# Attention on one core: Q and K of batches 1 to 7 transposed by the DMA crossbar instead of TensorE

## The chip, the core and the metric

The kernel runs on one core of a Trainium2 chip. Five engines of that core matter here: TensorE (PE, matmuls; its weight loads are listed as PEld), VectorE (DVE), ScalarE (ACT), GpSimd (POOL) and SyncE (SP). GpSimd and SyncE only issue DMAs in this kernel; 16 DMA engines move the data between HBM and SBUF, or inside SBUF. The metric is the device time of one execution in microseconds.

## The reference

The reference is plain attention without a mask, over 8 batches of 2048 rows with 512 columns, all float32.

```python
# q, k, v: (8, 2048, 512) float32
def reference(q, k, v):
    d_k = q.shape[-1]
    scores = np.matmul(q, k.transpose(0, 2, 1)) / np.sqrt(d_k)
    attn_weights = special.softmax(scores, axis=-1).astype(np.float32)
    return np.matmul(attn_weights, v)
```

## The kernel before

The batches are worked on one after another. A batch's 2048 rows are 16 blocks of 128 (NKB), its 512 columns four chunks of 128 (ND).

**Loads.** `prep_dma(b)` loads K, Q and V of a batch with GpSimd's DMAs (L62 to L64), which turn float32 into float16 on the way. K and Q come in two halves of eight blocks each, into the tiles `kh` and `qh`, of which there is one buffer each (`prep_pool`, bufs=1): the load of the next batch has to wait until the transposes of this one have read them. V comes into `vh`, with a column of ones behind it (L56), in two buffers.

**Transposes.** TensorE contracts over partitions, so the scores need Q and K with the columns (d) on the partitions. `prep_tr(b)` makes `qtT` and `ktT` from `qh` and `kh` (two buffers each). For each half, for K and then Q, and for each chunk of d, eight TensorE transposes against an identity matrix (L80) fill one PSUM tile `trp` (one buffer), and VectorE copies it to SBUF (L85). That is 16 groups of eight transposes for a batch.

**The main loop.** `main_batch(b)` goes over four query tiles (qt) of 512 rows. For each of them it does two stages:

- Scores: for each of the 16 key blocks four matmuls over the chunks of d (L98, 128 x 128 weights from `ktT`, 512 columns from `qtT`) give a tile `stp` in PSUM, and ScalarE writes exp of it, scaled, into `ptall` (L105). The softmax's maximum isn't subtracted.
- Output: for each of the four 128-row parts (qs) of the query tile, 16 pairs of matmuls (L117 with 257 columns, L121 with 256) sum exp times V, and through the column of ones the row sums, into a PSUM tile `op`, of which there are two buffers. VectorE takes the reciprocal of the sum (L126) and multiplies (L129) into `osb`, of which there are four buffers, and SyncE's queue stores it (L131).

`main_batch(b)` begins with `prep_dma(b + 1)`, and after query tile 1 it calls `prep_tr(b + 1)`. Batch 0 is loaded and transposed ahead of the loop.

**Order.** Each engine works its instructions in order, and so does each engine that issues DMAs: a DMA whose data isn't ready holds up the ones behind it in the same issuing engine's stream. The tile framework puts in the waits and may move instructions of one engine past each other by their readiness: in the trace the transposes of the next batch stand between the score matmuls of query tile 2, eight transposes to four score matmuls.

Of the kernel before, what the change touches and what calls it, by code (L numbers as in the profile page):

```python
# [1 line left out]

# [1 line left out]

# [5 lines left out]


@with_exitstack
def kernel(
    ctx: ExitStack,
    tc: tile.TileContext,
    q: bass.AP,
    k: bass.AP,
    v: bass.AP,
    out: bass.AP,  # L20
):
    nc = tc.nc
    P = 128
    B, T, D = q.shape
    F16 = mybir.dt.float16
    F32 = mybir.dt.float32

    NKB = T // P
    ND = D // P
    QTW = 512  # L30
    NQT = T // QTW
    NQS = QTW // P
    NB_ = 256
    NA_ = D + 1 - NB_
    inv_sqrt_d = float(1.0 / np.sqrt(D))
    GP = min(8, NKB)
    NG = NKB // GP

    const = ctx.enter_context(tc.tile_pool(name="const", bufs=1))
    prep_pool = ctx.enter_context(tc.tile_pool(name="prep", bufs=1))  # L40
    persist = ctx.enter_context(tc.tile_pool(name="persist", bufs=2))
    pt_pool = ctx.enter_context(tc.tile_pool(name="ptp", bufs=2))
    oout_pool = ctx.enter_context(tc.tile_pool(name="oout", bufs=4))
    st_psum = ctx.enter_context(tc.tile_pool(name="st_ps", bufs=3, space=bass.MemoryType.PSUM))
    o_psum = ctx.enter_context(tc.tile_pool(name="o_ps", bufs=2, space=bass.MemoryType.PSUM))
    tr_psum = ctx.enter_context(tc.tile_pool(name="tr_ps", bufs=1, space=bass.MemoryType.PSUM))

    ident = const.tile([P, P], F16)

    prepared = {}  # L50

    def prep_dma(b):
        qh = prep_pool.tile([P, NKB, D], F16, tag="qh")
        kh = prep_pool.tile([P, NKB, D], F16, tag="kh")
        vh = persist.tile([P, NKB, D + 1], F16, tag="vh")
        nc.vector.memset(vh[:, :, D:D + 1], 1.0)  # L56
        qsrc = q[b].rearrange("(n p) d -> p n d", p=P)
        ksrc = k[b].rearrange("(n p) d -> p n d", p=P)
        vsrc = v[b].rearrange("(n p) d -> p n d", p=P)
        for g in range(NG):  # L60
            ts = slice(g * GP, (g + 1) * GP)
            nc.gpsimd.dma_start(out=kh[:, ts, :], in_=ksrc[:, ts, :])  # L62
            nc.gpsimd.dma_start(out=qh[:, ts, :], in_=qsrc[:, ts, :])  # L63
        nc.gpsimd.dma_start(out=vh[:, :, 0:D], in_=vsrc)  # L64
        prepared[b] = [qh, kh, vh, None, None]

    def prep_tr(b):
        st = prepared[b]
        qh, kh = st[0], st[1]
        qtT = persist.tile([P, ND, T], F16, tag="qtT")  # L70
        ktT = persist.tile([P, ND, T], F16, tag="ktT")
        st[3] = qtT
        st[4] = ktT
        for g in range(NG):
            for src, dst in ((kh, ktT), (qh, qtT)):
                for dc in range(ND):
                    trp = tr_psum.tile([P, GP * P], F16, tag="trp")
                    for j in range(GP):
                        tb = g * GP + j
                        nc.tensor.transpose(  # L80
                            trp[:, j * P:(j + 1) * P],
                            src[:, tb, dc * P:(dc + 1) * P],
                            ident,
                        )
                    nc.vector.tensor_copy(  # L85
                        out=dst[:, dc, g * GP * P:(g + 1) * GP * P], in_=trp[:]
                    )

    def main_batch(b):
        if b + 1 < B:  # L90
            prep_dma(b + 1)
        _, _, vh, qtT, ktT = prepared[b]
        for qt in range(NQT):
            ptall = pt_pool.tile([P, NKB, QTW], F16, tag="ptall")
            for kb in range(NKB):
                stp = st_psum.tile([P, QTW], F32, tag="stp")
                for dc in range(ND):
                    nc.tensor.matmul(  # L98
                        stp[:],
                        ktT[:, dc, kb * P:(kb + 1) * P],  # L100
                        qtT[:, dc, qt * QTW:(qt + 1) * QTW],
                        start=(dc == 0),
                        stop=(dc == ND - 1),
                    )
                nc.scalar.activation(  # L105
                    out=ptall[:, kb, :],
                    in_=stp[:],
                    func=mybir.ActivationFunctionType.Exp,
                    scale=inv_sqrt_d,
                )  # L110
            for qs in range(NQS):
                op = o_psum.tile([P, 2 * 512], F32, tag="op")
                opA = op[:, 512:512 + NA_]
                opB = op[:, 0:NB_]
                for kb in range(NKB):
                    lhs = ptall[:, kb, qs * P:(qs + 1) * P]
                    nc.tensor.matmul(  # L117
                        opA, lhs, vh[:, kb, NB_:NB_ + NA_],
                        start=(kb == 0), stop=(kb == NKB - 1),
                    )  # L120
                    nc.tensor.matmul(  # L121
                        opB, lhs, vh[:, kb, 0:NB_],
                        start=(kb == 0), stop=(kb == NKB - 1),
                    )
                rinv = oout_pool.tile([P, 1], F32, tag="rinv")
                nc.vector.reciprocal(out=rinv[:], in_=op[:, 512 + NA_ - 1:512 + NA_])  # L126
                osb = oout_pool.tile([P, D], F32, tag="osb")
                src = op.rearrange("p (a c) -> p a c", c=512)[:, :, 0:NB_]
                nc.vector.tensor_scalar_mul(out=osb[:], in0=src, scalar1=rinv[:])  # L129
                gq = qt * NQS + qs  # L130
                nc.sync.dma_start(  # L131
                    out=out[b, gq * P:(gq + 1) * P, :], in_=osb[:]
                )
            if qt == min(1, NQT - 1) and b + 1 < B:
                prep_tr(b + 1)

    prep_dma(0)
    ident_dram = nc.inline_tensor(
        np.eye(P, dtype=np.float16), name="attn_identity"
    )  # L140
    nc.sync.dma_start(out=ident[:], in_=ident_dram.ap())
    prep_tr(0)
    for b in range(B):
        main_batch(b)


# [1 line left out]
_INS = ['q', 'k', 'v']  # L148
_OUTS = [((8, 2048, 512), 'float32')]


# [23 lines left out]
```

## Time and profile before

| what | value |
|---|---|
| median of the runs | 985.29 us |
| lowest of the runs | 985.02 us |
| span of the profiled execution | 983.6 us |
| granted TensorE clock, mean | 0.999 |
| TensorE busy | 963.9 us, 7168 matmuls and transposes |
| VectorE busy | 205.8 us |
| ScalarE busy | 306.7 us |
| HBM read, written | 100.70 MB, 33.55 MB |

The span runs from the first to the last instruction of one profiled execution, and its time on the device is slightly longer. In the groups of the page a row names the line, the engine and the operation, what is written and read with its shape, how often it ran, then its busy time in us, the mean of one in ns, and the idle time ahead of it with what ended it. In the rows of the timeline the first two numbers are the start and the length in us. In a row of DMA issues the last numbers are the size of one and the median time from issue to landing.

### The profile page before, as it was taken

How to read it: one execution, taken by the hardware profiler on the slowest of the kernel's cores; microseconds unless marked ns; L12 is line 12 of the kernel's file. 1: busy time of each engine (PE TensorE's matmuls, PEld its weight loads, DVE VectorE, ACT ScalarE, POOL GpSimd, SP SyncE). 2: the span in 40 equal slices, each digit the busy share in tenths (PEclk: the TensorE clock that was granted, in tenths of full speed). 3: DMA queues.
4: the chain of work that ended last, by engine and by line, in shares of the span. 5: the costliest groups of instructions: out<-in, count | busy, mean ns of one | idle time of the engine just before them, and what ended most of it. 6: DMA issues, size and time to landing. Idle time of an engine off the chain costs nothing.

```text
span 983.6 us, 15767 instructions
## 1 busy us (share of the span) xinstructions
PE 963.9 (98%) x7168; PEld 658.6 (67%) x7168; DVE 205.8 (21%) x392; ACT 306.7 (31%) x513; POOL 37.5 (4%) x44
## 2 busy tenths in 40 slices
PE   4999999999999999999999999999999999999998
PEld 3667766667666676666676766667666677666676
DVE  2214311142111421114111141112411123111111
ACT  0332233322233322233322233322333222333221
POOL 2100100001000000001000010000100000000000
PEclk9999999999999999999999999999999999999999
DMA  9991926009160192502934048521566110001111
GB/s 170 208 180 44 174 74 118 33 33 203 54 119 33 34 204 56 110 36 49 179 79 94 33 70 156 103 70 43 81 134 127 45 44 23 33 33 43 43 44 43
DMA packets 68435, 84.94 MB, mean 86 GB/s; under 512 B 2832, under 2 KB 51984, under 8 KB 68368
## 3 DMA queue, kind: packets, MB, share of 16 engines
q0 software_dynamic: 49792, 50.33, 32.2%
q1 hardware_dynamic: 18576, 33.60, 9.2%
q8 instruction: 56, 0.92, 0.4%
q14 instruction: 11, 0.09, 0.0%
HBM read 100.70 MB, written 33.55 MB: 136 GB/s over the span
## 4 chain that ended last, share of the span: by engine, by line
PE 98%; DMA 1%; DVE 1%; issue 0%; POOLq 0%
PE stp L98 45%; PE op L117 23%; PE op L121 23%; PE trp L80 7%; DMA kh<-in_k_dram 1%; DVE ktT L85 0%; DVE qtT L85 0%; DVE osb L129 0%; DVE rinv L126 0%; POOLq L159 0%
## 5 line engine op out<-in xcount | busy, mean ns | idle before, releaser
L105 ACT ACTIVATE ptall<-stp 128x512 f16<-128x512 f32 x512 | 305.5, 597 | 658.3 <-PE stp L98 658.3
L98 PE MATMUL stp<-qtT,ktT 128*128 128x512 f16 x2048 | 467.0, 380 | 0.0
L117 PE MATMUL op<-vh,ptall 128*128 128x257 f16 x2048 | 452.5, 273 | 0.0
L121 PE MATMUL op<-vh,ptall 128*128 128x256 f16 x2048 | 452.5, 272 | 0.0
L98 PEld LDWEIGHTS <-ktT 128*128 128x128 f16 x2048 | 195.6, 98 | 208.0 <-issue 0.6
L117 PEld LDWEIGHTS <-ptall 128*128 128x128 f16 x2048 | 198.8, 97 | 30.5
L121 PEld LDWEIGHTS <-ptall 128*128 128x128 f16 x2048 | 199.5, 97 | 28.8
L126 DVE RECIPROCAL rinv<-op 128x1 f32<-128x1 f32 x128 | 21.6, 168 | 672.0 <-PE op L121 672.0
L129 DVE TENSOR_SCALAR osb<-op,rinv 128x512 f32<-128x512 f32 x128 | 96.1, 751 | 4.5 <-DVE rinv L126 0.3
L80 PEld LDWEIGHTS <-kh 128*128 128x128 f16 x512 | 35.0, 100 | 31.1 <-issue 14.5
L85 DVE COPY ktT<-trp 128x1024 f16<-128x1024 f16 x64 | 44.2, 691 | 50.7 <-PE trp L80 50.7
L85 DVE COPY qtT<-trp 128x1024 f16<-128x1024 f16 x64 | 44.3, 692 | 46.3 <-PE trp L80 46.3
L80 PE MATMUL trp<-ident,kh 128*128 128x128 f16 x512 | 40.5, 224 | 13.7 <-DMA kh<-in_k_dram 10.3
L80 PEld LDWEIGHTS <-qh 128*128 128x128 f16 x512 | 34.9, 99 | 22.0 <-issue 14.8
L80 PE MATMUL trp<-ident,qh 128*128 128x128 f16 x512 | 40.1, 222 | 1.6 <-DVE ktT L85 0.8
L62 POOL DMA_DIRECT2D kh<-in_k_dram x16 | 14.2, 889 | 436.4 <-PE trp L80 435.6
L64 POOL DMA_DIRECT2D vh<-in_v_dram x8 | 9.2, 1153 | 248.3 <-DVE osb L129 207.1
L63 POOL DMA_DIRECT2D qh<-in_q_dram x16 | 14.0, 882 | 27.5 <-PE trp L80 27.5
L105 ACT ACT_TABLE_LOAD x1 | 1.3, 1283 | 0.7 <-PEq L159 0.7
L56 DVE MEMSET vh<- 128x16 f16 x8 | 0.6, 72 | 0.9 <-PEq L159 0.9
L159 POOL MEMSET const-float32-0.0<- 128x1 f32 x1 | 0.1, 98 | 0.2 <-issue 0.2
L159 POOL MEMSET const-bfloat16-1.0<- 128x1 bf16 x1 | 0.1, 101 | 0.0
(2 smaller groups left out, 0.2 us busy)
## 6 DMA issues: line engine op xcount, KB each, us to landing
out_dram<-osb SPq DMA_DIRECT2D x128, 256.0 KB, 2.0
kh<-in_k_dram POOLq DMA_DIRECT2D x16, 1024.0 KB, 14.2
qh<-in_q_dram POOLq DMA_DIRECT2D x16, 1024.0 KB, 21.5
vh<-in_v_dram POOLq DMA_DIRECT2D x8, 2048.0 KB, 14.8
ident<-attn_identity SPq DMA_DIRECT2D x1, 32.0 KB, 1.6
```

The source lines that it names most:

```text
L56: nc.vector.memset(vh[:, :, D:D + 1], 1.0)
L62: nc.gpsimd.dma_start(out=kh[:, ts, :], in_=ksrc[:, ts, :])
L63: nc.gpsimd.dma_start(out=qh[:, ts, :], in_=qsrc[:, ts, :])
L64: nc.gpsimd.dma_start(out=vh[:, :, 0:D], in_=vsrc)
L80: nc.tensor.transpose(trp[:, j * P:(j + 1) * P], src[:, tb, dc * P:(dc + 1) * P], ident,)
L85: nc.vector.tensor_copy(out=dst[:, dc, g * GP * P:(g + 1) * GP * P], in_=trp[:])
L98: nc.tensor.matmul(stp[:], ktT[:, dc, kb * P:(kb + 1) * P], qtT[:, dc, qt * QTW:(qt + 1) * QTW], start=(dc == 0), stop=(dc == ND - 1),)
L105: nc.scalar.activation(out=ptall[:, kb, :], in_=stp[:], func=mybir.ActivationFunctionType.Exp, scale=inv_sqrt_d,)
L117: nc.tensor.matmul(opA, lhs, vh[:, kb, NB_:NB_ + NA_], start=(kb == 0), stop=(kb == NKB - 1),)
L121: nc.tensor.matmul(opB, lhs, vh[:, kb, 0:NB_], start=(kb == 0), stop=(kb == NKB - 1),)
L126: nc.vector.reciprocal(out=rinv[:], in_=op[:, 512 + NA_ - 1:512 + NA_])
L129: nc.vector.tensor_scalar_mul(out=osb[:], in0=src, scalar1=rinv[:])
```

## The change

Q and K of batches 1 to 7 are no longer transposed by TensorE. `prep_tr(b)` for b > 0 issues eight transposing DMAs on SyncE's queue instead, SBUF to SBUF: four groups of four blocks (TG = 4), K and Q in turn, each with a source of 128 partitions x 2048 float16. Batch 0 is still transposed by TensorE, in groups of two blocks with all four chunks of d each.

`qtT` and `ktT` get another layout, [128, block, chunk, row in the block] instead of [128, chunk, row]; the score matmul's moving operand becomes four runs of 128 columns, 512 elements apart. The call of `prep_tr(b + 1)` moves from behind query tile 1 to behind query tile 0. Loads, output stage and stores stay as they are.

```diff
+    TG = 4
...
     def prep_tr(b):
         st = prepared[b]
         qh, kh = st[0], st[1]
-        qtT = persist.tile([P, ND, T], F16, tag="qtT")
-        ktT = persist.tile([P, ND, T], F16, tag="ktT")
+        qtT = persist.tile([P, NKB, ND, P], F16, tag="qtT")
+        ktT = persist.tile([P, NKB, ND, P], F16, tag="ktT")
         st[3] = qtT
         st[4] = ktT
-        for g in range(NG):
+        if b == 0:
+            for g in range(NG):
+                for src, dst in ((kh, ktT), (qh, qtT)):
+                    for j in range(0, GP, 2):
+                        tb = g * GP + j
+                        trp = tr_psum.tile([P, 2, ND, P], F16, tag="trp")
+                        for jj in range(2):
+                            for dc in range(ND):
+                                nc.tensor.transpose(
+                                    trp[:, jj, dc, :],
+                                    src[:, tb + jj, dc * P:(dc + 1) * P],
+                                    ident,
+                                )
+                        nc.vector.tensor_copy(out=dst[:, tb:tb + 2], in_=trp[:])
+            return
+        for g in range(NKB // TG):
+            ns = slice(g * TG, (g + 1) * TG)
             for src, dst in ((kh, ktT), (qh, qtT)):
-                for dc in range(ND):
-                    trp = tr_psum.tile([P, GP * P], F16, tag="trp")
-                    for j in range(GP):
-                        tb = g * GP + j
-                        nc.tensor.transpose(
-                            trp[:, j * P:(j + 1) * P],
-                            src[:, tb, dc * P:(dc + 1) * P],
-                            ident,
-                        )
-                    nc.vector.tensor_copy(
-                        out=dst[:, dc, g * GP * P:(g + 1) * GP * P], in_=trp[:]
-                    )
+                nc.sync.dma_start_transpose(
+                    out=dst[:, ns].rearrange("p n c r -> p (n c) r"),
+                    in_=src[:, ns, :].rearrange("p n d -> p (n d)"),
+                )
...
-                        ktT[:, dc, kb * P:(kb + 1) * P],
-                        qtT[:, dc, qt * QTW:(qt + 1) * QTW],
+                        ktT[:, kb, dc, :],
+                        qtT[:, qt * NQS:(qt + 1) * NQS, dc, :],
...
-            if qt == min(1, NQT - 1) and b + 1 < B:
+            if qt == 0 and b + 1 < B:
                 prep_tr(b + 1)
```

## The prediction

> **What bounds the kernel now.** I read the page's head and its chain of waits first, then the costliest groups.
>
> ```profile
> span 983.6 us, 15767 instructions
> PE 963.9 (98%) x7168; PEld 658.6 (67%) x7168; DVE 205.8 (21%) x392; ACT 306.7 (31%) x513; POOL 37.5 (4%) x44
> PE stp L98 45%; PE op L117 23%; PE op L121 23%; PE trp L80 7%; DMA kh<-in_k_dram 1%; DVE ktT L85 0%; DVE qtT L85 0%; DVE osb L129 0%; DVE rinv L126 0%; POOLq L159 0%
> ...
> L105 ACT ACTIVATE ptall<-stp 128x512 f16<-128x512 f32 x512 | 305.5, 597 | 658.3 <-PE stp L98 658.3
> ...
> L85 DVE COPY ktT<-trp 128x1024 f16<-128x1024 f16 x64 | 44.2, 691 | 50.7 <-PE trp L80 50.7
> ...
> L80 PE MATMUL trp<-ident,kh 128*128 128x128 f16 x512 | 40.5, 224 | 13.7 <-DMA kh<-in_k_dram 10.3
> ...
> L80 PE MATMUL trp<-ident,qh 128*128 128x128 f16 x512 | 40.1, 222 | 1.6 <-DVE ktT L85 0.8
> ```
>
> TensorE is the bound: 98% busy, and the chain of waits runs through it nearly end to end. Of that chain, 7% is L80, the 1024 transposes. The other engines are far away from it: ScalarE has 658.3 us of idle time, waiting for TensorE. So an instruction taken off TensorE in the steady part should come off the time whole. A busy sum is no price for it, since matmuls overlap; I take the price from stretches of batch 1, cut at the moments where VectorE begins the last reciprocal (L126) of a query tile (qt). The columns are the stretch, its length, then busy time and count of each engine, the granted clock, the DMA share and GB/s.
>
> ```profile
> 148.13:176.03 27.90, 27.90 (x193) 18.71 (x192) 3.71 (x10) 9.55 (x16) 1.15 (x1) 1.00 0.58 113
> 176.03:203.93 27.90, 27.90 (x196) 18.82 (x195) 3.68 (x9) 9.55 (x16) 0.00 (x0) 1.00 0.10 39
> 203.93:240.15 36.22, 36.22 (x321) 25.70 (x319) 14.65 (x25) 9.55 (x16) 3.49 (x4) 1.00 0.61 107
> ```
>
> A query tile without transposes takes 27.90 us, the one that holds the 128 transposes of the next batch 36.22 us; both at a granted clock of 1.00 and with TensorE never idle. One batch's transposes therefore cost 36.22 - 27.90 = 8.32 us, or 65 ns each.
>
> **The change part by part.** *Removed from TensorE:* the transposes of batches 1 to 7, 7 x 8.32 = 58.2 us, all of it on the path. The eviction copies of those batches go from VectorE too (112 x 0.69 us); VectorE is 21% busy, so that is worth nothing.
>
> *Batch 0* keeps 128 transposes and 16 evictions of the same size, in another order: two 128-row blocks with all four d chunks each, instead of one chunk of eight blocks.
>
> ```profile
> 12.13 1.01 PE L80 MATMUL trp<-ident,kh 128*128 128x128 f16 x8 [0.78 <-DVE ktT L85]
> ...
> 19.31 1.01 PE L80 MATMUL trp<-ident,qh 128*128 128x128 f16 x8 [0.78 <-DVE qtT L85]
> ...
> 20.12 1.48 PE L98 MATMUL stp<-qtT,ktT 128*128 128x512 f16 x3
> ```
>
> Before, the first score matmuls fill the gaps after six groups of eight. After, the first score tile needs the first K pair and two Q pairs, which is again the sixth group in order. I take 0; one or two groups earlier or later, at 1.79 us each (1.01 + 0.78), bound it at 3.6 us to either side.
>
> *The score matmul's moving operand* becomes four runs of 128 columns instead of one of 512. No row shows such an operand.
>
> ```profile
> 35.08 6.91 PE stp L98 x32
> ```
>
> This row of the chain gives 6.91 / 32 = 216 ns for the run of 512. Four separate 128-column matmuls at the 65 ns above would be 260 ns, so +44 ns x 2048 = 90 us is the upper end. The lower end is 0: TensorE issues these back to back and the columns stay as many. I take 0, as the same elements of the same partitions are streamed.
>
> *Added on SP's queue:* 8 transposing DMAs a batch, 56 in all, each 128 x 2048 f16 = 512 KB in and out of SBUF, placed behind the outputs of qt 0 and ahead of those of qt 1. Call the time of one T and of a batch X = 8T. No row shows a crossbar transfer; these are the nearest.
>
> ```profile
> DMA packets 68435, 84.94 MB, mean 86 GB/s; under 512 B 2832, under 2 KB 51984, under 8 KB 68368
> q0 software_dynamic: 49792, 50.33, 32.2%
> q1 hardware_dynamic: 18576, 33.60, 9.2%
> out_dram<-osb SPq DMA_DIRECT2D x128, 256.0 KB, 2.0
> kh<-in_k_dram POOLq DMA_DIRECT2D x16, 1024.0 KB, 14.2
> ident<-attn_identity SPq DMA_DIRECT2D x1, 32.0 KB, 1.6
> ```
>
> Lower end: the hardware queue's packets took 9.2% of 16 engines x 983.6 us = 1448 us for 33.60 MB, 371 GB/s when all 16 run; 512 KB at that rate is 1.4 us. Upper end: a 128x128 block of f16 is 32 KB in 128 rows of 256 bytes, just what the identity's load is, and that took 1.6 us; 16 such blocks, each waiting for the one before, are 25.6 us. Between them lies the store of 256 KB on the same queue: 2.0 us to landing, so 4.0 us for 512 KB as two of them. I take T = 4.0 us, X = 32 us, because that row is nearest in queue, engines and size, and both its latencies are already counted.
>
> Here two pages of the Trainium skill disagree. "DMA: Bandwidth & Descriptors" (section Latency and other measured facts) gives 261 GB/s for transposing DMAs whose middle dimension isn't contiguous; as an estimate that is T = 2.0 us, as hidden as mine. "VectorE: DVE Perf Modes" (section The three transpose paths) sets 1309 ns for a 128x128 block by the crossbar against 390 ns on TensorE, and would leave such a block to TensorE; 16 of those in a row are an estimate of 20.9 us. The identity's 1.6 us for one small DMA reads like such a figure: mostly latency, which 16 blocks in one DMA don't each pay.
>
> *What hides X.* SP works in order, so qt 1's outputs stand behind the eight transposes. VectorE's L129 waits for an osb buffer (4 of them), the op buffers in PSUM (2) then stay full, and TensorE's L117 stops. When, the rows of batch 1 tell.
>
> ```profile
> 176.03 0.17 DVE L126 RECIPROCAL rinv<-op 128x1 f32<-128x1 f32 x1 [2.57 <-PE op L121]
> 176.23 0.75 DVE L129 TENSOR_SCALAR osb<-op,rinv 128x512 f32<-128x512 f32 x1
> 193.36 0.17 DVE L126 RECIPROCAL rinv<-op 128x1 f32<-128x1 f32 x1 [16.38 <-PE op L121]
> ...
> 196.88 0.17 DVE L126 RECIPROCAL rinv<-op 128x1 f32<-128x1 f32 x1 [2.57 <-PE op L121]
> ```
>
> ```profile
> 204.91 0.33 SPq L131 DMA_DIRECT2D out_dram<-osb  x1
> ```
>
> The last output of qt 0 is ready at 176.23 + 0.75 = 177.0; there the transposes start. Their issue, taken as that of a store, is 8 x 0.33 = 2.6 us of SP's time, inside X. The four outputs of qt 1 fill the four osb buffers. Without transposes qt 2 follows 27.90 us behind qt 1: its first result is ready at 193.36 + 27.90 = 221.3, its second at 196.88 + 27.90 = 224.8, and there TensorE wants the first op buffer again. To free it in time VectorE must begin by 224.8 - 0.9 = 223.9 (0.17 + 0.75), so the first delayed output must have landed by then; with its own 2.0 us, X may be up to 223.9 - 2.0 - 177.0 = 45 us, T up to 5.6 us. Beyond that each us costs TensorE a us, in each of batches 0 to 6. With X = 32 us the slack is 13 us. The other deadline, scores of the next batch, comes later: three query tiles after qt 0 are 83.7 us.
>
> *What the transposes wait for* is the load of kh and qh, with SP's outputs behind that wait. The loads' stretches, batch 1's first:
>
> ```profile
> 60.00:65.00 5.00, 5.00 (x25) 2.28 (x24) 0.00 (x0) 3.40 (x7) 0.00 (x0) 1.00 1.21 229
> 65.00:70.00 5.00, 5.00 (x26) 2.38 (x25) 0.00 (x0) 3.40 (x7) 0.00 (x0) 1.00 0.85 141
> 70.00:75.00 5.00, 5.00 (x47) 4.41 (x46) 0.92 (x2) 0.52 (x1) 0.00 (x0) 1.00 0.00 0
> ...
> 130.00:140.00 10.00, 10.00 (x75) 7.17 (x74) 0.92 (x2) 3.31 (x6) 0.00 (x0) 1.00 0.06 24
> ```
>
> ```profile
> 100.41 1.76 POOL L62 DMA_DIRECT2D kh<-in_k_dram  x2 [62.41 <-PE trp L80]
> ```
>
> Batch 1 has landed by 70, inside qt 1 of batch 0, before that tile's first output; half of the transposes can run earlier. From batch 2 on a load starts when the transposes before it are done (kh and qh have one buffer) and takes some 30 us (100.4 to 130). After the change it starts in qt 2 of the batch before and lands about 20 us ahead of its transposes. I cost this wait at 0.
>
> *Sum:* 983.6 - 58.2 = 925.4 us of span. The median of the runs, 985.29, lies 1.7 us above the span; with the same 1.7 the forecast is 927.
>
> **The rivals.** *Outputs stuck behind slow transposes (slower).* The rows of 256 bytes could cost what packets cost on this queue: 1448 us / 18576 = 78 ns each, although they average 1.8 KB; the software queue's 1 KB packets take 102 ns (32.2% of 15738 us / 49792), so the price doesn't shrink with the bytes. 2048 rows over 16 engines are 128 each, T = 10 us, X = 80, stall 80 - 45 = 35 us in seven batches: 927 + 245 = 1172 us. It turns from gain to loss at X = 45 + 8.3 = 53 us, T = 6.7. Against it: SBUF to SBUF there is no HBM at either end. Chance of a T over 7.0 us: 0.22, of which 0.08 lies at T up to 8 (X = 64, 19 x 7 = 133, 1060 us), 0.10 around 1172, and 0.04 for blocks that go one at a time: T = 25.6, X = 205, 927 + 7 x 160 = 2047 us. The Trainium skill's 20.9 us (above) would be its milder form.
>
> *Partly hidden.* T from 5.6 to 7.0 us: stalls of 0 to 11 us a batch, 927 to 1005 us. For it: the margin is only 13 us of 45. Chance 0.08, of which 0.05 within 2%.
>
> *The four-run operand costs TensorE time.* At the upper end above, 927 + 90 = 1017 us; it decides from 58.2 / 2048 = 28 ns a matmul. Chance 0.04, nearly all against, since the operand before steps through SBUF the same within each run.
>
> *Hidden,* my forecast: 0.66.
>
> **How the numbers follow.** A measurement of this kernel tells about 2% from no change, so faster means below 965.6 and slower above 1005. Faster: 0.66 + 0.03 = 0.69. Same: 0.05. Slower: 0.22 + 0.04 = 0.26. The likeliest case alone gives 922 to 935 us (3.6 us for batch 0, some us of stall). The range must reach further to hold 8 in 10: 0.66 + 0.08 + 0.08 up to 1060 us, with the operand's case inside it. Low 921, high 1060.
>
> **What would show it.** Right: L80 falls from 1024 to 128, every query tile of batches 1 to 7 takes 27.9 us, TensorE stays at 98%, and the crossbar DMAs land within 4 us each once they run, SP's outputs of qt 1 late but no L117 idle time. Wrong: L117 or L129 idle behind out_dram once a batch in qt 2 (X over 45 us); stp idle behind the crossbar DMA at a batch's start; L98's spacing over 216 ns; outputs of qt 1 held by a wait for kh or qh. A mean of a crossbar DMA above 6.7 us would make the forecast's sign wrong.

## The result and the profile after

The kernel after the change takes 936.45 us in the median of its runs, beside 985.25 us before: a ratio of 0.950, with a 95% interval of 0.949 to 0.952. It is faster by 48.8 us. The forecast was 927. One of the four runs before took 1723.77 us, and the ratio leaves it out.

The page of the profiled execution after the change, cut to its bound, its chain of waits, the groups that changed and the DMA issues:

```profile
span 934.5 us, 13963 instructions
PE 909.8 (97%) x6272; PEld 610.8 (65%) x6272; DVE 128.8 (14%) x280; ACT 306.9 (33%) x513; POOL 37.5 (4%) x44
PEclk9998999999999999999999999999999999999999
...
PE stp L107 44%; PE op L126 23%; PE op L130 23%; DMA kh<-in_k_dram 4%; SPq L93 3%; DMA out_dram<-osb 0%; DVE osb L138 0%; POOL kh L63 0%; POOL qh L64 0%; SPq L140 0%; DVE rinv L135 0%; POOLq L63 0%; DVEq L138 0%; POOLq L168 0%; POOLq L64 0%
L126 PE MATMUL op<-vh,ptall 128*128 128x257 f16 x2048 | 455.3, 274 | 5.1 <-DVE osb L138 5.1
...
L138 DVE TENSOR_SCALAR osb<-op,rinv 128x512 f32<-128x512 f32 x128 | 96.1, 751 | 26.5 <-DMA out_dram<-osb 22.4
...
out_dram<-osb SPq DMA_DIRECT2D x128, 256.0 KB, 2.6
...
ktT<-kh SPq DMA_TRANSPOSE x28, 4.9
qtT<-qh SPq DMA_TRANSPOSE x28, 5.7
```

The rows of the output matmul and of VectorE's product before, for comparison:

```profile
L117 PE MATMUL op<-vh,ptall 128*128 128x257 f16 x2048 | 452.5, 273 | 0.0
...
L129 DVE TENSOR_SCALAR osb<-op,rinv 128x512 f32<-128x512 f32 x128 | 96.1, 751 | 4.5 <-DVE rinv L126 0.3
```

TensorE has 896 instructions fewer, all of them transposes, and it is still the bound. (Line numbers moved: L107 is the score matmul, L126 and L130 the output pair, L135 and L138 VectorE's reciprocal and product, L140 the store, L93 the crossbar DMA.) Three things are new: the chain goes through SP's queue at L93 and through the load of K; the output matmul sat idle for 5.1 us behind VectorE's L138 (0.0 before); and L138 sat idle for 26.5 us, 22.4 of them behind the stores (4.5 us before, none behind a store). The row of the clock says where: its fourth slice, 70 to 93 us.

Stretches of the same execution, cut again at reciprocals: first the query tile 1 of batch 0 in four pieces, then a query tile of batch 0 and one of the last batch. (The DMA share, the last column but one, adds up the times of all packets, so it can pass 1.)

```profile
56.98:74.31 17.33, 17.33 (x98) 9.47 (x97) 0.92 (x2) 9.55 (x16) 0.00 (x0) 1.00 1.24 188
74.31:81.35 7.04, 3.48 (x32) 2.83 (x30) 0.17 (x1) 0.00 (x0) 0.00 (x0) 0.99 1.11 221
81.35:89.28 7.93, 6.49 (x32) 4.45 (x32) 1.49 (x4) 0.00 (x0) 0.51 (x1) 0.58 1.12 190
89.28:93.15 3.87, 3.73 (x33) 3.23 (x34) 0.91 (x3) 0.00 (x0) 2.08 (x3) 1.00 0.95 148
...
121.05:148.95 27.90, 27.90 (x193) 18.68 (x192) 3.68 (x8) 9.55 (x16) 0.00 (x0) 1.00 0.58 101
...
816.60:844.50 27.90, 27.90 (x195) 18.72 (x193) 3.68 (x8) 9.55 (x16) 0.00 (x0) 1.00 0.10 38
```

In the steady part a query tile takes 27.90 us, as it did without transposes before, so the 58.2 us are saved in full there. In batch 0 the pieces from 74.31 to 93.15 us, 18.84 us, do the work of three output parts of 3.52 us, 10.56 us: 8.3 us are lost. TensorE is idle for 7.04 - 3.48 + 7.93 - 6.49 + 3.87 - 3.73 = 5.1 us of them; the remaining 3.2 us go with a granted clock of 0.58 after the idle stretch.

The span is 934.5 us where the forecast had 925.4. Of the 9.1 us, 8.3 are this one stall; the other 0.9 us lies at the start, where the first reciprocal begins at 46.41 us instead of 45.54.

The timelines of SP and of VectorE after the change show what happens there:

```profile
51.79 19.23 SPq L93 DMA_TRANSPOSE ktT<-kh  x2
71.06 4.34 SPq L93 DMA_TRANSPOSE qtT<-qh  x2
75.45 2.90 SPq L93 DMA_TRANSPOSE ktT<-kh  x1
78.40 0.60 SPq L140 DMA_DIRECT2D out_dram<-osb  x1
```

```profile
57.18 0.75 DVE L138 TENSOR_SCALAR osb<-op,rinv 128x512 f32<-128x512 f32 x1
74.31 0.17 DVE L135 RECIPROCAL rinv<-op 128x1 f32<-128x1 f32 x1 [16.38 <-PE op L130]
81.47 0.75 DVE L138 TENSOR_SCALAR osb<-op,rinv 128x512 f32<-128x512 f32 x1 [6.99 <-DMA out_dram<-osb]
```

The first store of the whole kernel leaves SP at 78.40 us, though its data was ready at 47.4. Ahead of it stand five crossbar DMAs of batch 1. The first of them waits for K of batch 1 until 51.79, which is 4.4 us of the store's delay of 31 us; the other 26.6 us are SP's time for the five. The first two alone take 19.23 us of it, while the loads of batch 1 fill the DMA engines. The four results of query tile 0 hold the four osb buffers meanwhile, the last since 57.18, and so VectorE can't write the fifth until 81.47.

The diff puts the crossbar DMAs behind the stores of query tile 0. In the program the tile framework has moved them ahead. With the call of `prep_tr` put back behind query tile 1 the instruction streams of all engines come out as they are, so that edit of the change has no effect (this is read from the program; no run was made of it). The wait at the head of a later batch's crossbar DMAs isn't for a load; of SP's waits at L93 one is for K's load, until 51.79, and six are for the scores at L107:

```profile
246.46 1.80 SPq L93 DMA_TRANSPOSE ktT<-kh  x1
248.37 2.39 SPq L93 DMA_TRANSPOSE qtT<-qh  x1
250.82 2.85 SPq L93 DMA_TRANSPOSE ktT<-kh  x1
253.75 0.61 SPq L140 DMA_DIRECT2D out_dram<-osb  x1
254.42 3.67 SPq L93 DMA_TRANSPOSE qtT<-qh  x1
258.18 1.98 SPq L93 DMA_TRANSPOSE ktT<-kh  x1
260.25 0.92 SPq L140 DMA_DIRECT2D out_dram<-osb  x1
261.25 3.25 SPq L93 DMA_TRANSPOSE qtT<-qh  x1
264.56 8.54 SPq L93 DMA_TRANSPOSE ktT<-kh  x1
273.19 0.53 SPq L140 DMA_DIRECT2D out_dram<-osb  x1
273.78 8.34 SPq L93 DMA_TRANSPOSE qtT<-qh  x1
```

They start at 246.46 us, at the end of the last scores of batch 1, which frees the buffers of `qtT` and `ktT`. Batch 3's transposes so run beside the last outputs of batch 1 and in query tile 0 of batch 2, and end at 282.1 us, ahead of the last outputs of that tile (288.5), behind which the source calls them. And three stores stand between them. SP's time is 1.8 to 3.7 us for each of the first six, and 8.3 to 8.5 us for the last two. A batch takes 273.78 + 8.34 - 246.46 = 35.7 us with its three stores, close to the 32 us of the forecast.

### The profile page after: what moved, and what is told of

The parts are those of the page before. It is cut to its first block, busy times and chain, and to the rows that moved or that the text cites. A ratio compares the mean times of both kernels' runs of the same rounds, so it can differ in the third digit from the quotient of the medians.

```text
span 934.5 us, 13963 instructions
## 1 busy us (share of the span) xinstructions
PE 909.8 (97%) x6272; PEld 610.8 (65%) x6272; DVE 128.8 (14%) x280; ACT 306.9 (33%) x513; POOL 37.5 (4%) x44
## 4 chain that ended last, share of the span: by engine, by line
PE 90%; DMA 5%; SPq 3%; issue 1%; POOL 0%; DVE 0%; POOLq 0%; DVEq 0%
PE stp L107 44%; PE op L126 23%; PE op L130 23%; DMA kh<-in_k_dram 4%; SPq L93 3%; DMA out_dram<-osb 0%; DVE osb L138 0%; POOL kh L63 0%; POOL qh L64 0%; SPq L140 0%; DVE rinv L135 0%; POOLq L63 0%; DVEq L138 0%; POOLq L168 0%; POOLq L64 0%
## 5 line engine op out<-in xcount | busy, mean ns | idle before, releaser
L126 PE MATMUL op<-vh,ptall 128*128 128x257 f16 x2048 | 455.3, 274 | 5.1 <-DVE osb L138 5.1
L130 PE MATMUL op<-vh,ptall 128*128 128x256 f16 x2048 | 455.2, 273 | 0.0
L107 PE MATMUL stp<-qtT,ktT 128*128 128x512 f16 x2048 | 450.5, 380 | 0.0
L107 PEld LDWEIGHTS <-ktT 128*128 128x128 f16 x2048 | 200.4, 98 | 233.4 <-issue 1.1
L126 PEld LDWEIGHTS <-ptall 128*128 128x128 f16 x2048 | 199.6, 97 | 36.9 <-DVE osb L138 5.7
L130 PEld LDWEIGHTS <-ptall 128*128 128x128 f16 x2048 | 200.2, 98 | 29.4
L135 DVE RECIPROCAL rinv<-op 128x1 f32<-128x1 f32 x128 | 21.5, 168 | 749.4 <-PE op L130 749.4
L138 DVE TENSOR_SCALAR osb<-op,rinv 128x512 f32<-128x512 f32 x128 | 96.1, 751 | 26.5 <-DMA out_dram<-osb 22.4
L83 PE MATMUL trp<-ident,kh 128*128 128x128 f16 x64 | 6.6, 266 | 12.8 <-DMA kh<-in_k_dram 10.5
L83 PEld LDWEIGHTS <-kh 128*128 128x128 f16 x64 | 5.6, 123 | 14.8 <-DMA kh<-in_k_dram 10.5
L83 PE MATMUL trp<-ident,qh 128*128 128x128 f16 x64 | 6.5, 262 | 2.3 <-DVE qtT L88 1.6
L83 PEld LDWEIGHTS <-qh 128*128 128x128 f16 x64 | 5.6, 120 | 4.7 <-issue 4.2
L88 DVE COPY ktT<-trp 128x1024 f16<-128x1024 f16 x8 | 5.5, 691 | 17.5 <-PE trp L83 17.5
L88 DVE COPY qtT<-trp 128x1024 f16<-128x1024 f16 x8 | 5.5, 691 | 8.0 <-PE trp L83 8.0
```

What stands on the lines that cost most here:

```text
L83: nc.tensor.transpose(trp[:, jj, dc, :], src[:, tb + jj, dc * P:(dc + 1) * P], ident,)
L88: nc.vector.tensor_copy(out=dst[:, tb:tb + 2], in_=trp[:])
L107: nc.tensor.matmul(stp[:], ktT[:, kb, dc, :], qtT[:, qt * NQS:(qt + 1) * NQS, dc, :], start=(dc == 0), stop=(dc == ND - 1),)
L126: nc.tensor.matmul(opA, lhs, vh[:, kb, NB_:NB_ + NA_], start=(kb == 0), stop=(kb == NKB - 1),)
L130: nc.tensor.matmul(opB, lhs, vh[:, kb, 0:NB_], start=(kb == 0), stop=(kb == NKB - 1),)
```

## The experiments

The theory is: 8.3 of the 9.1 us are one stall in batch 0, made by SP's order, the four osb buffers and the loads of batch 1. Its first rival is that loads and crossbar traffic slow the engines there, whatever the order; its second, that the new operand or the new order of batch 0 costs time. Each edit is against the kernel after the change.

**Eight osb buffers.**

```diff
-    oout_pool = ctx.enter_context(tc.tile_pool(name="oout", bufs=4))
+    oout_pool = ctx.enter_context(tc.tile_pool(name="oout", bufs=8))
```

> Eight osb buffers in place of four, nothing else. Theory (stall): VectorE no longer waits for out_dram in query tile 1 of batch 0, so TensorE doesn't either, though the stores still stand behind the crossbar DMAs: 928 us (926 to 930), clock 1.00 there. Rival (traffic): 934 to 937, as the same bytes move at the same time.

Measured: 927.45 us, ratio 0.941 (0.940 to 0.943) to the kernel before; span 925.3. The query tile 1 of batch 0 in its stretches, and SP's first store in its timeline:

```profile
56.11:84.01 27.90, 27.90 (x193) 18.69 (x192) 3.67 (x9) 9.55 (x16) 0.00 (x0) 1.00 1.20 193
```

```profile
78.62 0.60 SPq L140 DMA_DIRECT2D out_dram<-osb  x1
```

The store is as late as before (78.62), the DMA engines as busy (share 1.20), and yet the query tile takes 27.90 us at a clock of 1.00. The stall is the wait for an osb buffer; the traffic rival falls. This is also what the forecast's sum described, with nothing stalled: 925.4 of span and 927 us. The first reciprocal starts at 45.54 us here, as before the change, so the 0.9 us at the start belong neither to the new order nor to the operand; starts of 45.5 to 46.4 us occur in the runs with the same code ahead of them. TensorE's rows show where most of it arises: the first score matmuls run at about half speed, 1.91 us for four, and the full speed, 1.03 us for four, comes at different moments. The second four take 1.91 us after the change (from 24.63 us) and 1.28 us here (from 24.50). The runs that begin at 46.2 us, those with batch 1 or all batches by TensorE, have 1.89 and 1.78 us at that place. What sets the moment stays open.

The control, the kernel before with eight osb buffers:

> The kernel before with eight osb buffers. In its trace VectorE never waits for out_dram, so the buffers alone give nothing: 984.5 to 986 us. Rival (more buffers help any order): 980 us or less.

Measured: 985.73 us, ratio 1.000 (0.999 to 1.001). The buffers pay only where the stores are held up.

**The stores on ScalarE's queue.**

```diff
-                nc.sync.dma_start(
+                nc.scalar.dma_start(
                     out=out[b, gq * P:(gq + 1) * P, :], in_=osb[:]
```

> The stores of the output go to ScalarE's queue; SP keeps the crossbar DMAs alone. Theory (stall): the 9.1 us that the span has over 925.4 are one stall in batch 0, where the first outputs stand on SP behind crossbar DMAs that wait for batch 1's K (5.1 us of idle TensorE, 3.2 us of lower clock after it) and 0.9 us at the start. Then query tile 1 of batch 0 takes 27.9 us, L126 has no idle time, the granted clock is 1.00 there, and the time is 928 us (926 to 930). Rival (traffic): loads and crossbar DMAs together slow TensorE or VectorE in the first 100 us, whatever queue the stores are on; then query tile 1 of batch 0 stays at 36 us and the time at 934 to 937.

Measured: 950.64 us, ratio 0.964 (0.963 to 0.966): slower than the change. Both expectations missed. Two rows of its waits (who waited for whom: total us, times, longest) and two of ScalarE's timeline:

```profile
ACT ptall L114 <- DMA qtT<-qh: 37.3, 2, 34.6
...
PE stp L107 <- ACT ptall L114: 20.7, 2, 19.2
```

```profile
46.62 30.62 ACTq L140 DMA_DIRECT2D out_dram<-osb  x3
77.28 0.60 ACT L114 ACTIVATE ptall<-stp 128x512 f16<-128x512 f32 x1 [34.58 <-DMA qtT<-qh]
```

The first store leaves at once (46.62), but those behind it wait for crossbar DMAs of the other queue: in the program the second store waits for a semaphore that an earlier DMA of SP sets, since eight semaphores serve the DMAs of both queues in turn. The exp of query tile 1 stands behind those stores, and TensorE waits 19.2 us for it. The stores' wait moved from SP's queue to ScalarE's; it didn't go away.

**Batch 1 by TensorE too.**

```diff
-        if b == 0:
+        if b <= 1:
             for g in range(NG):
```

> Batch 1 too is transposed by TensorE; the crossbar takes batches 2 to 7. Theory (stall): 8.3 us of transposes come back and the 8.3 us of the stall go: 934 to 938 us, with no idle time of L126 and no clock below 0.99 after the start. Rival (traffic): the loss of the first 100 us stays in part, since the loads are the same: 940 to 945 us.

Measured: 936.09 us, ratio 0.950 (0.949 to 0.951); L126 has no idle time and the mean clock is 1.000 (0.996 after the change). The 8.3 us of transposes came back and the 8.3 us of stall went, as the theory said.

**Everything by TensorE, with the new layout.**

```diff
-        if b == 0:
+        if True:
             for g in range(NG):
```

> All batches transposed by TensorE, but with the new layout, the new order of the groups and the four-run operand: the change without the crossbar. Theory (stall): the operand costs nothing and the order 0.9 us at the start: 985 to 987 us, L98's 64 score matmuls at 13.81 us a query tile. Rival (operand): part of the missing 9 us is the operand; each ns of it is 2 us, so 990 us or more.

Measured: 985.76 us, ratio 1.000 (0.999 to 1.001). The operand of four runs and the new order of the groups together cost nothing within some 1 us, and the gain and the stall are the crossbar's.

**V of batch 0 alone.**

```diff
-        vh = persist.tile([P, NKB, D + 1], F16, tag="vh")
-        nc.vector.memset(vh[:, :, D:D + 1], 1.0)
+        if b == 0:
+            vh = persist.tile([P, NKB, D + 1], F16, tag="vh")
+            nc.vector.memset(vh[:, :, D:D + 1], 1.0)
+        else:
+            vh = prepared[0][2]
...
-        nc.gpsimd.dma_start(out=vh[:, :, 0:D], in_=vsrc)
+        if b == 0:
+            nc.gpsimd.dma_start(out=vh[:, :, 0:D], in_=vsrc)
```

> Only V of batch 0 is loaded and all batches use it (the output of batches 1 to 7 is not attention with their own V). The 2 MB of batch 1's V no longer go ahead of its K and Q, with four osb buffers as in the change. Theory (late loads are what makes SP's order cost something): K and Q of batch 1 land some 10 us earlier, the first store of batch 0 leaves SP before 70 us in place of 78.4, VectorE finds its osb buffer free, and the span is 925 to 927 us though seven crossbar DMAs now stand ahead of that store. Rival (the order alone costs it): the stall of some 8 us stays, 934 us.

Measured, in a single run: 941.78 us, span 940.0; the expectation missed. SP's timeline:

```profile
41.15 24.85 SPq L97 DMA_TRANSPOSE ktT<-kh  x4
66.04 14.54 SPq L97 DMA_TRANSPOSE qtT<-qh  x3
80.69 0.51 SPq L144 DMA_DIRECT2D out_dram<-osb  x1
```

K of batch 1 is there 10 us earlier (41.15), and still the first store leaves at 80.69, behind seven crossbar DMAs instead of five; TensorE waits 13.0 us. So earlier loads alone don't help. But the edit moved the order as well, and while the crossbar DMAs ran the loads went on (with K of batch 2 issued at 68.8 us already); how much of the stall the lateness of the loads makes with the order as in the change stays open.

**Each crossbar DMA twice.**

```diff
-                nc.sync.dma_start_transpose(
-                    out=dst[:, ns].rearrange("p n c r -> p (n c) r"),
-                    in_=src[:, ns, :].rearrange("p n d -> p (n d)"),
-                )
+                for _ in range(2):
+                    nc.sync.dma_start_transpose(
+                        out=dst[:, ns].rearrange("p n c r -> p (n c) r"),
+                        in_=src[:, ns, :].rearrange("p n d -> p (n d)"),
+                    )
```

> Each crossbar DMA is issued twice onto the same tile, so a batch has 16 of them, X of some 60 to 76 us. The model of the prediction (all of a batch's crossbar DMAs in one block ahead of four outputs, 45 us of cover): stalls of 15 to 30 us in each of seven batches, 1040 to 1150 us. Theory (outputs stand between the crossbar DMAs in SP's stream, so each waits for two or three of them only): batches 1 to 6 stay at 27.9 us a query tile, and only batch 0, where the loads are late, stalls longer: 945 to 980 us.

Measured, in a single run: 954.29 us, span 952.5. The first and the last of batch 2's crossbar DMAs in SP's timeline, and a stretch of 27.90 us beside them (cut by the clock, not at reciprocals):

```profile
151.38 1.80 SPq L94 DMA_TRANSPOSE ktT<-kh  x1
...
208.13 2.52 SPq L94 DMA_TRANSPOSE qtT<-qh  x1
```

```profile
193.00:220.90 27.90, 26.73 (x181) 17.25 (x179) 3.58 (x8) 9.55 (x16) 3.50 (x4) 1.00 1.13 209
```

X is 208.13 + 2.52 - 151.38 = 59 us, 14 us above the cover of 45 us that the prediction worked out, but TensorE is idle for 1.2 us only, and not at all in later batches; the query tile beside their end takes 29.40 us (193.37 to 222.77), 1.5 more than the others. So the block of the prediction, a whole batch of crossbar DMAs ahead of four outputs, isn't what runs. That the stores between them make the cover longer is the likely reason, and no run tests it by itself. Of the 18 us over the change, 16.6 are in batch 0: its query tile 1 takes 38.04 us (36.17 in the change) and its query tile 2 takes 42.61 (27.90).

**Larger and smaller crossbar DMAs.**

```diff
-    TG = 4
+    TG = 8
```

and the same with TG = 2.

> TG = 8: four crossbar DMAs of 1 MB a batch in place of eight of 512 KB. If SP's time for one goes by its 16-row blocks (256 instead of 128): 3.6 to 5.2 us each when no load runs, the batch's sum unchanged. If it is a fixed price of a DMA: 1.8 to 2.6 us each, the sum halved. Time 932 to 940 us either way.

> TG = 2: sixteen crossbar DMAs of 256 KB a batch. By blocks: 0.9 to 1.3 us of SP each when no load runs, the sum unchanged. By a fixed price: 1.8 to 2.6 us each, the sum doubled. Time 930 to 945 us either way.

Measured, one run each: 944.42 us and 936.14 us. SP's time for one, least, median and most in ns, from the rows of L93 in both:

```profile
L93 SPq DMA_TRANSPOSE ktT<-kh x14: 4788/5133/19256, 51.8 to 711.7; - x14
```

```profile
L93 SPq DMA_TRANSPOSE ktT<-kh x56: 1231/1336/7884, 52.1 to 727.0; - x56
```

Medians of 5.1 us for 1 MB and 1.3 us for 256 KB, beside 2.6 us for 512 KB in the change: SP's time goes by size, and nothing fixed shows in it. To landing the least are 6.8, 3.1 and 4.4 us, so some 2 us stand there beside what goes by size. The 944 us of TG = 8 lie beyond what was expected; there the first store leaves at 81.0 us, and L126 waits 12.6 us instead of 5.1.

**V loaded for two batches only.**

```diff
-        vh = persist.tile([P, NKB, D + 1], F16, tag="vh")
-        nc.vector.memset(vh[:, :, D:D + 1], 1.0)
+        if b < 2:
+            vh = persist.tile([P, NKB, D + 1], F16, tag="vh")
+            nc.vector.memset(vh[:, :, D:D + 1], 1.0)
+        else:
+            vh = prepared[b - 2][2]
...
-        nc.gpsimd.dma_start(out=vh[:, :, 0:D], in_=vsrc)
+        if b < 2:
+            nc.gpsimd.dma_start(out=vh[:, :, 0:D], in_=vsrc)
```

> V is loaded for batches 0 and 1 only, and later batches use those two tiles again (the output of batches 2 to 7 is not attention with their own V). Theory: the crossbar DMAs that take 8 to 10 us in the kernel after the change are those that share the DMA engines with V's load; without it all of batches 2 to 7 take 2 to 4 us of SP, and a batch's eight fit in 30 us instead of 38. Rival: they are slow for another reason (the semaphores of earlier stores, their place in the row): the two slow ones stay. Time 934 to 937 us in both, as no wait of TensorE hangs on them.

Measured, in a single run: 936.52 us. The same batch's last two crossbar DMAs in SP's timeline, beside the 8.54 and 8.34 us above:

```profile
264.26 1.99 SPq L97 DMA_TRANSPOSE ktT<-kh  x1
266.35 0.94 SPq L144 DMA_DIRECT2D out_dram<-osb  x1
267.34 3.01 SPq L97 DMA_TRANSPOSE qtT<-qh  x1
```

Without V's load they are as quick as the others, so it was V's load beside them that made them slow. The batch's eight now take 246.72 to 270.35 us, 23.6 us.

**A faster start.** Eight osb buffers, and batch 0's K and Q loaded in pieces of two blocks (of four in the second run):

```diff
-        for g in range(NG):
-            ts = slice(g * GP, (g + 1) * GP)
+        GL = 2 if b == 0 else GP
+        for g in range(NKB // GL):
+            ts = slice(g * GL, (g + 1) * GL)
```

> Eight osb buffers, and batch 0's K and Q loaded in eight pieces of two blocks each in place of two of eight, so that the first transpose need not wait for 1 MB. The first transpose starts at about 4 us instead of 10.3; the loads' rate then holds the rest up, so 3 to 5 us are gained on the eight buffers alone: 922 to 925 us. Rival (the loads' rate, not their first landing, sets the start): 926 to 928 us.

> As the run before with four pieces of four blocks: 923 to 926 us; the rival says 926 to 928.

Measured: 926.33 us, ratio 0.940 (0.939 to 0.941), and 925.95 us, ratio 0.940 (0.938 to 0.941). The intervals overlap with that of the eight buffers alone, so no gain over it is shown, and the 3 to 5 us expected of pieces of two weren't there. The timeline of TensorE with pieces of two says why:

```profile
5.54 1.03 PE L84 MATMUL trp<-ident,kh 128*128 128x128 f16 x8 [5.54 <-DMA kh<-in_k_dram]
8.36 1.04 PE L84 MATMUL trp<-ident,kh 128*128 128x128 f16 x8 [1.78 <-DMA kh<-in_k_dram]
10.92 1.04 PE L84 MATMUL trp<-ident,kh 128*128 128x128 f16 x8 [1.53 <-DMA kh<-in_k_dram]
```

The first group starts 4.8 us earlier, but the next three wait for the loads, and the first reciprocal comes only 1.3 us earlier (44.28 beside 45.54). The version to keep is the change with eight osb buffers; all three are faster than both kernels.

## Why the prediction was right, and where it was not

The time lies in the range, but 9 us above the forecast and just outside the 922 to 935 us of the likeliest case: the sum held in the steady part, and one wait that it had at nothing came in batch 0.

- *What TensorE loses.* 7 x 8.32 us was right: every query tile after batch 0 takes 27.90 us, and with the stall taken out the span is 925.3 us against 925.4.
- *Batch 0's order and the four-run operand at 0.* Right, shown by the run with all transposes on TensorE (985.76 us). The first score matmul does come one group later (22.07 us after, 20.12 before), but the first reciprocal doesn't (45.54 with eight buffers, as before).
- *T = 4.0 us, X = 32 us.* Near by luck: 35.7 us for a batch, but for other reasons than the row it came from. Undisturbed, one takes SP 1.8 to 3.9 us; from batch 2 on two in each batch take 8 to 10 us beside V's load, a sharing that the prediction left out. To landing, which is what the row of the store gave, one takes 4.4 us at least and 7.7 in the mean of the 56 (from the trace), so neither sign that the prediction named, within 4 us each or a mean above 6.7 and the sign wrong, came out: the landings overlap, and SP's time, 4.2 us in the mean, sets X. Both rivals for T fall as the price of all of them, 10 us by packets and 25.6 us block by block. As to the two pages of the Trainium skill: the effective rate of 261 GB/s in "DMA: Bandwidth & Descriptors" (Latency and other measured facts) is a quarter above what SP's time gives without V's load, 512 KB in some 2.5 us, 208 GB/s; the 1309 ns for one block in "VectorE: DVE Perf Modes" (The three transpose paths) doesn't carry over, since 16 blocks in one DMA cost SP about twice that together.
- *SP's time.* Taken as that of a store, 0.33 us a crossbar DMA; it is 2.6 us in the median for K and 3.3 us for Q (1780 and 2058 ns at least). Inside X it changed no sum, but SP issues nothing else meanwhile.
- *Where they stand in SP's stream.* Wrong: "placed behind the outputs of qt 0 and ahead of those of qt 1" took the source's order for the program's. They run from the moment the buffers come free, and in batch 0 ahead of the first store. This is the step that cost the 8.3 us: that store left SP 31 us late, 26.6 of them for the five crossbar DMAs ahead of it, at up to 11.5 us each beside the loads of batch 1.
- *The wait for kh and qh at 0.* Wrong, and the rest of that delay, 4.4 us: batch 1 had landed by 71 us, much as the rows said, but the stores that stood behind the wait were those of query tile 0, ready from 47.4 us, and not those of query tile 1. The named mechanism, four osb buffers full, then two op buffers, then the output matmul (L117 before, L126 after) idle, is the one that struck; it struck once, in batch 0, and not in seven batches.
- *The cover of 45 us.* Not reached in the steady part, and too short as a bound: 59 us fit with 1.2 us of idle time in the order that runs.

## What to carry to other kernels

Transposes that lie on a TensorE that never rests are worth their full time, and the crossbar hides them where a batch's transfers fit behind the work of the batch before. Look in the program, not in the source, for what stands behind the moved DMAs on the issuing engine, above all in the first iteration, where their inputs are late; where small results pile up behind them, more result buffers helped here (927.45 us) and another queue didn't (950.64 us), since it waited for the same semaphores. Take the price of a transfer at the place where it runs, beside the other transfers that run there.

## What the runs showed of the hardware

An idle stretch of TensorE costs more than its length. After 4.48 us of idle time (to 82.28 us, after the change) the granted clock is 0.50, and it is back at 1.00 by 89.4 us. The columns are as in the stretches above:

```profile
78.00:82.30 4.30, 0.02 (x1) 0.03 (x2) 0.82 (x2) 0.00 (x0) 0.00 (x0) 0.88 1.10 229
...
83.00:85.00 2.00, 2.00 (x11) 1.39 (x10) 0.00 (x0) 0.00 (x0) 0.00 (x0) 0.50 0.96 182
...
89.40:91.00 1.60, 1.58 (x15) 1.40 (x16) 0.03 (x1) 0.00 (x0) 0.25 (x1) 1.00 1.07 267
91.00:93.00 2.00, 2.00 (x21) 1.77 (x19) 0.75 (x1) 0.00 (x0) 1.56 (x2) 1.00 0.88 53
```

2 us at that clock touch 11 matmuls, and 2 us at the full clock, from 91.00 us on, touch 21. The Trainium skill, "TensorE: Matmul & The Clock Gate" (Part 1, The HAM clock gate), says that an idle window of about 3.4 us halves the clock and that about as long a busy one restores it; this trace agrees on the half and on an idle stretch of that size, and shows some 5.8 us until it is whole again (a mean of 0.78 from 87.00 to 89.40 us puts the rise from 0.50 to 1.00 at about 88.1). With eight buffers, the same transfers and no idle stretch, the clock stays at 1.00, so it is the idle time and not the traffic that lowers it. At the start the matmuls are as slow (after the change eight transposes in 1.01 us at 12.29, later in 0.61), though the granted clock reads 1.00 from 10 us on, so that column doesn't show everything.

A crossbar DMA takes longer when loads run beside it: 1.8 to 3.9 us of SP for 512 KB alone or beside stores, 8 to 10 us beside V's load, and 19.2 us for the first two, beside the loads of batch 1. Its traffic of 256-byte rows did not slow TensorE: 27.90 us a query tile, with DMA shares from 0.10 to 1.20.
